# The convolution norm: sums of squares as rows, the inverse root spread through memory

## The chip, the cores and the metric

The kernel runs on one core of one Trainium2 chip. The metric is device time in microseconds (us) of one execution; lower is better. Three runs of the kernel before took 2366.22, 2369.10 and 2373.38 us. The engines are named as the profile names them: PE (matrix products), PEld (its weight loads), DVE, ACT and POOL (elementwise work), SP (the queue that issues most of the transfers).

## The reference

One decoder block over 2048 tokens of 1024 channels, all in float32. The part that matters here is the convolution branch behind the depthwise convolution:

```python
def layer_norm(x, w, b):
    xf = x.astype(jnp.float32)
    mu = jnp.mean(xf, axis=-1, keepdims=True)
    var = jnp.mean(jnp.square(xf - mu), axis=-1, keepdims=True)
    return (xf - mu) * lax.rsqrt(var + EPS) * w.astype(jnp.float32) + b.astype(jnp.float32)
...
        u = a * jax.nn.sigmoid(b)
        u = depthwise_causal_conv(u, conv_w, conv_b)
        u = jax.nn.silu(layer_norm(u, conv_ln_w, conv_ln_b)).astype(dt)
        u = u * jax.nn.silu(g_conv)
        y_conv = u @ w_conv_out
...
        y_attn = o @ w_attn_out
        y = jax.nn.sigmoid(m_conv) * y_conv + jax.nn.sigmoid(m_attn) * y_attn
        out = y @ w_out
```

Per token there is one mean and one variance over 1024 channels, an inverse root of the variance, and then 1024 products with it.

## The kernel before, in words

Activations are kept transposed: channels lie on the 128 partitions, tokens along the row. A product in float32 accuracy is made of three products of halves of the numbers (a high part and a low part), so each matrix product appears three times.

The change lies in the last third of the program. There the tokens are cut into four quarters of 512 (t = 0 to 3), and two loops of 32 blocks each follow one another.

* **The ya loop** (the attention projection): block 8t + dm is 12 products (`project`, L1399) for the quarter t and 128 output channels dm; DVE then makes `yt` from the block's bank and a loaded tile `ma`, and SP stores `yt`.
* **The yc loop** (the convolution projection): block 8t + dm is 24 products on the tiles `u0`...`u7` (high `h`, low `l`) of the quarter t; DVE makes `mc` from the bank and a loaded tile `mc`, adds it to a loaded `yl`, and SP stores `yl`.

Both loops take their banks by dm from three names (z, s, o) with two banks each, so a block can start when the work on an earlier block's bank is done on DVE: in the ya loop block 24 takes the bank of block 19, for example. The tiles `ma` and `mc` have three buffers, `yl` four, `gg` (the silu gate's input of the norm) three. SP issues its transfers strictly in the order written, and waits in place when a buffer is not yet free or a value not yet there.

The convolution norm is made inside these loops, by the class `Norm`, one object for each quarter. Its steps are:

* `load`: the convolution's output `d` comes from memory (two buffers, so quarter t + 2 waits for quarter t);
* `mean` (L1421 to L1429): a product with ones gives the sums (`pm`), DVE takes the mean off, ACT squares, DVE sums the eight squares into `red`, which holds for each token 128 partial sums on 128 partitions;
* `variance` (L1435 to L1437, and L114, L115): four products with `red` as the weights and a column of ones turn `red` into a column of 128 tokens each (`pc`), DVE copies it to `stf`, POOL takes the power -1/2 (`rsqrt_cols`, two instructions);
* `spread` (L1444, L1447): four products with the column stretched over 128 columns and the identity give the inverse root on all 128 partitions (`pr`), ACT copies it to `rs`;
* `apply(k)` for k = 0 to 7 (L1452 to L1461): DVE multiplies `d` by `rs` (`vf`), ACT takes silu (`tv`), DVE multiplies by `gg` (`vf` again), ACT makes the high part `u_kh`, DVE the low part `u_kl`.

Where a step stands among the products is set by `at_block(n, m, f)`: step f is written ahead of product m of block n. On PE the program's order is kept as written. On DVE, ACT, POOL and SP the builder orders the instructions by its own estimate of when each can start, and the order is then fixed. Quarters 0 and 1 have their steps in the ya loop, quarters 2 and 3 in the yc loop; quarter 0 must be ready for yc block 0, quarter 1 for block 8, quarter 2 for block 16, quarter 3 for block 24. Beside the norm, DVE, ACT and SP prepare the weights of the final product in yc blocks 10 to 30 (`wo_raw`, `wot`, `woB`).

## Time and profile before

| what | value |
|---|---|
| runs shown | 2366.22, 2369.10, 2373.38 us, median 2369.1 |
| profiled execution | 2370.1 us, of it span 2368.3 us |
| granted clock of PE, mean | 0.997 |
| PE, DVE, ACT, POOL busy in the span | 98%, 73%, 43%, 35% |
| ya loop | about 1928 to 2027 us of the span |
| yc loop | about 2027 to 2212 us |

The span is the time from the first to the last instruction; the rest of the execution lies outside it. In the tables a line such as L1399 is a line of the kernel before, "idle" is time in which an engine did nothing ahead of an instruction, and the releaser is what ended that wait. "xN" counts records; one float32 product of full width makes two of them.

### The profile page before, as it was taken

The page shows a single profiled execution, that of the slowest core. Times are in us where ns is not written, and L with a number is a line of the kernel's source. Part 1 is how long each engine was busy: PE and PEld are TensorE (multiplying, and loading weights), DVE is VectorE, ACT ScalarE, POOL GpSimd, SP SyncE. Part 2 cuts the span into 40 slices and gives each one's busy share as a digit, 9 for nine tenths or more (in the row PEclk, how much of TensorE's full clock was granted, in tenths as well). Part 3 has the DMA queues.
Part 4 walks back from the last instruction along what each step waited for, and adds up shares of the span by engine and source line. Part 5 has one row for each costly group of instructions (what it writes and reads, how often), then busy time and mean ns, then how long its engine had stood idle before and what let it go on. Part 6 is the DMA issues. An engine that isn't in the chain of part 4 may idle for free.

```text
span 2368.3 us, 38785 instructions
## 1 busy us (share of the span) xinstructions
PE 2325.8 (98%) x12421; PEld 2083.0 (88%) x12421; DVE 1737.0 (73%) x4104; ACT 1020.9 (43%) x2825; POOL 836.1 (35%) x976
## 2 busy tenths in 40 slices
PE   6999999999999999999999999999999999999999
PEld 4899999999999999997888888788888888878887
DVE  7855655555556777776699999989968768787654
ACT  5733343343344555456444444544444444332221
POOL 4321111111111111123677778656556730000221
PEclk9999999999999999999999999999999999999999
DMA  7733544454552222144535445745444569876552
GB/s 279 241 116 117 160 125 144 149 169 149 158 162 67 60 80 67 47 123 154 170 135 176 160 152 195 241 130 151 139 150 134 165 213 330 292 236 204 185 167 102
DMA packets 354121, 378.57 MB, mean 160 GB/s; under 512 B 27688, under 2 KB 249176, under 8 KB 353918
## 3 DMA queue, kind: packets, MB, share of 16 engines
q1 hardware_dynamic: 312622, 314.05, 42.6%
q10 hardware_dynamic: 41296, 62.05, 7.5%
q8 instruction: 99, 1.62, 0.3%
q14 instruction: 104, 0.85, 0.1%
HBM read 235.34 MB, written 140.64 MB: 159 GB/s over the span
## 4 chain that ended last, share of the span: by engine, by line
PE 88%; DMA 4%; DVE 4%; ACT 2%; issue 1%; POOL 1%; SPq 0%; ACTq 0%; DVEq 0%; POOLq 0%
PE pz L549 31%; PE paab L1091 7%; PE yc L1399 6%; PE oa L1681 4%; PE pcab L1091 4%; PE pag_mc_d L1091 4%; PE pag_g_d L1091 3%; PE pag_ma_d L1091 3%; PE po L684 3%; PE ps L635 3%; PE ya L1399 2%; PE pcg_g_d L1091 2%; PE oc L1681 2%; PE pbab L1091 2%; PE paag L1091 2%; PE pcg_mc_d L1091 2%
## 5 line engine op out<-in xcount | busy, mean ns | idle before, releaser
L549 PE MATMUL pz<-wh_u,hT_lo 128*128 128x384 f32 x1504 | 525.2, 349 | 2.5 <-DVE hT_lo L371 2.4
L549 PE MATMUL pz<-wh_u,hT_hi 128*128 128x384 f32 x1504 | 505.6, 336 | 1.3 <-ACT hT_hi L369 1.3
L549 PE MATMUL pz<-wl_u,hT_hi 128*128 128x384 f32 x1504 | 505.8, 336 | 0.0
L114 POOL TENSOR_SCALAR st<-st 128x2 f32<-128x2 f32 x192 | 44.9, 234 | 797.0 <-ACT sq L572 796.7
L586 DVE SCALAR_TENSOR_TENSOR qk<-pz,st,wqk 128x128 f32<-128x128 f32 x384 | 116.9, 346 | 265.0 <-POOL st L115 260.8
L549 PEld LDWEIGHTS pz<-wh_u,hT_lo 128*128 128x128 f32 x1504 | 283.2, 188 | 4.0 <-DVE hT_lo L371 3.7
L549 PEld LDWEIGHTS pz<-wh_u,hT_hi 128*128 128x128 f32 x1504 | 283.8, 189 | 2.2 <-ACT hT_hi L369 1.9
L549 PEld LDWEIGHTS pz<-wl_u,hT_hi 128*128 128x128 f32 x1504 | 282.8, 188 | 0.5 <-issue 0.5
L627 ACT ACTIVATE qkT<-ptq 128x256 f32<-128x256 f32 x192 | 73.8, 384 | 358.1 <-PE ptq L620 302.5
L1169 DVE SCALAR_TENSOR_TENSOR ce<-us,pair_taps,ce 128x512 f32<-128x512 f32 x240 | 180.9, 754 | 6.5
L1140 DVE SCALAR_TENSOR_TENSOR ce<-ut,chan,ce 128x512 f32<-128x512 f32 x240 | 179.8, 749 | 0.0
L1055 POOL TENSOR_TENSOR slT<-wT,shT 128x512 fp32r<-128x512 f32 x107 | 143.8, 1345 | 79.8 <-ACT shT L1054 79.5
L1153 DVE SCALAR_TENSOR_TENSOR cq<-ut,chan,cq 128x512 f32<-128x512 f32 x208 | 156.0, 750 | 1.0
L1054 ACT ACTIVATE shB<-wB 128x512 fp32r<-128x512 f32 x130 | 82.1, 631 | 161.7 <-PE paab L1091 51.7
L115 POOL TENSOR_TENSOR st<-st,mhalf 128x2 f32<-128x2 f32 x192 | 140.1, 729 | 15.9
L572 ACT ACTIVATE sq<-pz 128x128 bf16<-128x128 f32 x384 | 106.1, 276 | 78.7 <-PE pz L549 68.9
L1054 ACT ACTIVATE shT<-wT 128x512 fp32r<-128x512 f32 x110 | 69.4, 631 | 160.9 <-POOL wT L1046 32.0
L1055 POOL TENSOR_TENSOR slB<-wB,shB 128x512 fp32r<-128x512 f32 x85 | 111.9, 1317 | 76.1 <-ACT shB L1054 73.8
L684 PE MATMUL po<-lv,pT 128*128 128x128 f32 x596 | 96.8, 274 | 0.0
L684 PEld LDWEIGHTS po<-lv,pT 128*128 128x128 f32 x596 | 90.9, 190 | 0.6 <-issue 0.5
L593 DVE TENSOR_TENSOR t<-qk,tab 128x256 f32<-128x256 f32 x192 | 82.5, 430 | 5.7
L1055 POOL TENSOR_TENSOR slT<-wB,shT 128x512 fp32r<-128x512 f32 x57 | 75.1, 1324 | 28.4 <-ACT shT L1054 28.3
(783 smaller groups left out, 6163.2 us busy)
## 6 DMA issues: line engine op xcount, KB each, us to landing
wB<-in_w_in_dram SPq DMA_DIRECT2D x154, 256.0 KB, 3.2
qkv_d<-qkv SPq DMA_DIRECT2D x128, 192.0 KB, 2.3
wT<-tT_d SPq DMA_DIRECT2D x88, 256.0 KB, 2.7
tT_d<-wB ACTq DMA_DIRECT2D x66, 256.0 KB, 2.7
lqk<-qkv_d SPq DMA_DIRECT2D x128, 128.0 KB, 2.3
raw_u<-in_w_in_dram SPq DMA_DIRECT2D x84, 192.0 KB, 3.6
acc_d<-osb SPq DMA_DIRECT2D x128, 65.0 KB, 2.0
part<-acc_d ACTq DMA_DIRECT2D x64, 130.0 KB, 2.4
```

Source lines behind the costliest of these rows:

```text
L115: nc.gpsimd.tensor_tensor(dst, scratch[:, :n], mhalf[:, :n], op=ALU.pow)
L549: nc.tensor.matmul(pz[:, :width], part(a, k, P * j, P), w[:, :width], start=(m == 0), stop=(m == 23))
L586: nc.vector.scalar_tensor_tensor(qk[:, 2 * i : 2 * i + 2].rearrange("p a b -> p (a b)"), pz[:, P * i : P * i + P], st[:, 2 + i : 3 + i], w ...
L684: nc.tensor.matmul(po[:, :P], box["pT"][:, P * i : P * i + P], vt, start=(i == 0), stop=(i == nk - 1))
L1054: nc.scalar.activation(h, q[name], AF.Copy)
L1055: eng.tensor_tensor(l, q[name], h.bitcast(F32), op=ALU.subtract)
L1091: nc.tensor.matmul(ps, w, x, start=(m == 0 and ps.name not in first), stop=(m == 11 and not more), skip_group_check=True)
L1140: stt(box["e"], e[:, 1 + j : 513 + j], chan[:, cb, 2 * j : 2 * j + 1], box["e"], op0=ALU.mult, op1=ALU.add)
L1153: stt(box["o"], o[:, 2 + j : 514 + j], w, psum_o, op0=ALU.mult, op1=ALU.add)
L1169: stt(dst, box["both"][:, 1 + j : 513 + j], pair_taps[:, cb, j : j + 1], box["e"], op0=ALU.mult, op1=ALU.subtract if j == 0 else ALU.add)
L1399: nc.tensor.matmul(pz, w, xx, start=(m == 0), stop=(m == len(terms) - 1))
L1681: nc.tensor.matmul(ps, y, w, start=(m == 0 and ps.name not in begun), stop=(m == 11 and not more), skip_group_check=True)
```

## The change

The sums of squares are made the other way round. Ones (32 columns of them) are now the weights, and a piece of `red` with 128 tokens is what streams: each of the four products gives a row of 128 sums, repeated on 32 partitions, and the four lie on partitions 0, 32, 64 and 96 of one bank. DVE copies the bank to `row`. Then memory does the rest: four writes of one row each make a line of 512 values in `var_d`, one read brings it back as 128 x 4 (`stf`), POOL takes the inverse root of that, one write puts it into a second line of 512, and one read copies that line to all 128 partitions (`rs`). The four identity products and ACT's copy are gone. All seven transfers are issued by SP.

POOL's two instructions now belong to `spread`. The steps stand at other places in the yc loop: `spread` of quarter 2 six products later in block 7, `variance` of quarter 3 in block 15 ahead of product 6 (it was block 14, product 12), `spread` of quarter 3 in block 16. The eight `apply` of quarter 2 go from 9.0 to block 14 in steps of 19 products (they stood in blocks 8 to 15, one in each), those of quarter 3 from block 17 to 22 in steps of 18.

```diff
+    var_d = [[dram.tile([512], F32, name=f"var{i}{t}_d") for i in range(2)] for t in range(S // 512)]
...
             pc = bank("t", f"pc{t}")
             for i in range(4):
-                nc.tensor.matmul(pc[:, i : i + 1], self.red[:, P * i : P * i + P], ones[:, :1], start=True, stop=True)
-            st = self.st = ap.tile([P, 12], F32, tag="stf", name=f"stf{t}")
-            nc.vector.tensor_copy(st[:, :4], pc[:, :4])
+                nc.tensor.matmul(pc[32 * i : 32 * i + 32, :P], ones[:, :32], self.red[:, P * i : P * i + P], start=True, stop=True)
+            row = ap.tile([P, P], F32, tag="row", name=f"row{t}", bufs=1)
+            nc.vector.tensor_copy(row, pc[:, :P])
+            for i in range(4):
+                nc.sync.dma_start(var_d[t][0][None, P * i : P * i + P], row[32 * i : 32 * i + 1, :])
+            self.st = ap.tile([P, 12], F32, tag="stf", name=f"stf{t}")
+            nc.sync.dma_start(self.st[:, :4], var_d[t][0].rearrange("(p i) -> p i", i=4))
+
+        def spread(self):
+            t, st = self.t, self.st
             rsqrt_cols(st[:, 4:8], st[:, :4], 4, st[:, 8:12])
-
-        def spread(self):
-            t = self.t
-            pr = bank("t", f"pr{t}")
-            for i in range(4):
-                nc.tensor.matmul(pr[:, P * i : P * i + P], self.st[:, 4 + i : 5 + i].to_broadcast([P, P]), ident,
-                                 start=True, stop=True)
+            nc.sync.dma_start(var_d[t][1].rearrange("(p i) -> p i", i=4), st[:, 4:8])
             self.rs = ap.tile([P, 512], F32, tag="rs", name=f"rs{t}")
-            nc.scalar.activation(self.rs, pr, AF.Copy)
+            nc.sync.dma_start(self.rs, var_d[t][1][None, :].to_broadcast([P, 512]))
...
-                    (8, 3, "load"), (9, 3, "mean"), (14, 3, "variance"), (15, 3, "spread")):
+                       (8, 12, 3, "load"), (9, 12, 3, "mean"), (15, 6, 3, "variance"), (16, 12, 3, "spread")):
...
-            at_block(KC * (t - 1) + k, 17, lambda t=t, k=k: norms[t].apply(k))
+            at = 24 * KC * (t - 1) + (17 + 24 * k if t == 1 else 24 + 19 * k if t == 2 else 36 + 18 * k)
+            at_block(at // 24, at % 24, lambda t=t, k=k: norms[t].apply(k))
```

Outside the norm's surroundings all engines keep their order. POOL's order is the same throughout. Three places show what moved. In the names the first digit is the quarter, the second the block or the k; a number behind the last underscore only tells buffers apart.

On PE, around quarter 3's variance, before (yc blocks 14 and 15):

```order
L1399 MATMUL yc1_6_24492<-u1_3l_23987,wc1h0_23759 128x512
L1399 MATMUL yc1_6_24492<-u1_3h_23986,wc1l0_23761 128x512
L1435 MATMUL pc3_24505<-ones_92,red3_24255 128x1 x4
L1399 MATMUL yc1_6_24492<-u1_4h_24029,wc1h1_23760 128x512
L1399 MATMUL yc1_6_24492<-u1_4l_24030,wc1h1_23760 128x512
...
L1399 MATMUL yc1_7_24544<-u1_3h_23986,wc1l0_23761 128x512
L1444 MATMUL pr3_24557<-ident_87,stf3_24510 128x128 x4
L1399 MATMUL yc1_7_24544<-u1_4h_24029,wc1h1_23760 128x512
```

and the same place on PE after:

```order
L1400 MATMUL yc1_7_24560<-u1_1h_23896,wc1h0_23771 128x512
L1400 MATMUL yc1_7_24560<-u1_1l_23897,wc1h0_23771 128x512
L1400 MATMUL yc1_7_24560<-u1_1h_23896,wc1l0_23773 128x512
L1436 MATMUL pc3_24567<-red3_24269,ones_100 32x128 x4
L1400 MATMUL yc1_7_24560<-u1_2h_23947,wc1h0_23771 128x512
L1400 MATMUL yc1_7_24560<-u1_2l_23948,wc1h0_23771 128x512
```

The four `pc3` stand 18 products later, in block 15, and the four `pr3` are gone.

On SP, ahead of yc blocks 9 to 12, before (stores `y_d<-yl`, loads of `mc`, `yl` and of quarter 2's `gg`):

```order
L1654 DMA yl1_1_24238<-ya_d_81 128x512
L1661 DMA y_d_82<-yl0_6_24088 128x512
L1652 DMA mc1_1_24236<-mc_d_77 128x512
L1654 DMA yl1_2_24314<-ya_d_81 128x512
L1452 DMA gg2_3_24377<-g_d_76 128x512
L1452 DMA gg2_4_24424<-g_d_76 128x512
L1661 DMA y_d_82<-yl0_7_24140 128x512
L1652 DMA mc1_2_24312<-mc_d_77 128x512
L1654 DMA yl1_3_24357<-ya_d_81 128x512
```

and after (`d3` is quarter 3's load, `var02_d` and `var12_d` are quarter 2's two lines in memory):

```order
L1440 DMA var02_d_91<-row2_24120 1x128 x4
L1416 DMA d3_24219<-u_d_75 128x2x512
L1664 DMA y_d_82<-yl0_6_24100 128x512
L1416 DMA d3_24219<-u_d_75 128x2x512
L1442 DMA stf2_24126<-var02_d_91 128x4
L1655 DMA mc1_1_24239<-mc_d_77 128x512
...
L1664 DMA y_d_82<-yl0_7_24156 128x512
L1655 DMA mc1_2_24326<-mc_d_77 128x512
L1447 DMA var12_d_92<-stf2_24126 128x4
L1657 DMA yl1_3_24371<-ya_d_81 128x512
L1664 DMA y_d_82<-yl1_0_24204 128x512
L1449 DMA rs2_24191<-var12_d_92 128x512
```

The seven small transfers now stand among the stores and loads of blocks 6 to 11, and the loads of quarter 2's `gg` from k = 3 on stand behind them.

On DVE, where quarter 2's last parts and quarter 3's last sum of squares are made, before:

```order
L1461 TENSOR_TENSOR u2_6l_24527<-vf2_6_24521,u2_6h_24526 128x512
L1429 TENSOR_TENSOR red3_24255<-red3_24255,sq3_6_24279 128x512
L1660 TENSOR_TENSOR yl1_4_24400<-yl1_4_24400,mc1_4_24398 128x512
L1461 TENSOR_TENSOR u2_7l_24577<-vf2_7_24571,u2_7h_24576 128x512
L1429 TENSOR_TENSOR red3_24255<-red3_24255,sq3_7_24283 128x512
```

and after:

```order
L1463 TENSOR_TENSOR u2_2l_24353<-vf2_2_24347,u2_2h_24352 128x512
L1430 TENSOR_TENSOR red3_24269<-red3_24269,sq3_7_24297 128x512
L1463 TENSOR_TENSOR u2_3l_24391<-vf2_3_24385,u2_3h_24390 128x512
...
L1438 COPY row3_24572<-pc3_24567 128x128
L1456 SCALAR_TENSOR_TENSOR vf2_7_24533<-d2_23757,chan_113,rs2_24191 128x512
L1460 SCALAR_TENSOR_TENSOR vf2_6_24495<-tv2_6_24497,gg2_6_24493 128x512
L1460 SCALAR_TENSOR_TENSOR vf2_7_24533<-tv2_7_24535,gg2_7_24531 128x512
L1463 TENSOR_TENSOR u2_6l_24501<-vf2_6_24495,u2_6h_24500 128x512
L1662 SCALAR_TENSOR_TENSOR mc1_7_24556<-mc1_7_24556,yc1_7_24560 128x512
L1463 TENSOR_TENSOR u2_7l_24539<-vf2_7_24533,u2_7h_24538 128x512
```

Quarter 3's last sum now comes when quarter 2 has its parts up to k = 2, and quarter 2's last part stands behind `mc` of block 15, one block ahead of its use; from quarter 2's first `vf` (the instruction behind quarter 3's mean on DVE) to that last sum there are 29 instructions, to the last part 48.

4 lines of the change are left out of this document (2 added, 2 removed).

## The prediction, on record before the run

> **What bounds the kernel now.** I read the page's engine shares and its chain first, then the list of what PE waited for, then the stages around the change, then the chain itself there.
>
> ```profile
> PE 2325.8 (98%) x12421; PEld 2083.0 (88%) x12421; DVE 1737.0 (73%) x4104; ACT 1020.9 (43%) x2825; POOL 836.1 (35%) x976
> ...
> PE 88%; DMA 4%; DVE 4%; ACT 2%; issue 1%; POOL 1%; SPq 0%; ACTq 0%; DVEq 0%; POOLq 0%
> ```
>
> PE is busy for 98% of the span and is 88% of the chain that ended last. So a PE instruction taken away is worth its time, and anything else is worth only what PE waits for it.
>
> ```profile
> PE paab L1091 <- ACT spare_hi L1217: 4.1, 1, 4.1
> ...
> PE pc L1435 <- DVE red L1429: 2.8, 1, 2.8
> ...
> PE ptq L620 <- DVE lqk L596: 2.2, 1, 2.2
> ...
> PE pr L1444 <- POOL stf L115: 0.4, 1, 0.4
> ```
>
> Columns: total wait, times, longest. Two of PE's waits stand in the steps that change: 2.8 us for a `red`, 0.4 us for POOL.
>
> ```profile
> 1966.00:2027.00 61.00, 60.64 (x281) 49.95 (x280) 47.82 (x79) 24.82 (x40) 3.38 (x4) 1.00 0.93 312
> 2027.00:2083.00 56.00, 56.00 (x252) 45.90 (x251) 46.10 (x75) 23.61 (x38) 1.26 (x2) 1.00 0.84 278
> 2083.00:2125.00 42.00, 39.16 (x174) 32.26 (x173) 36.12 (x55) 11.46 (x19) 1.63 (x2) 0.96 0.72 243
> ```
>
> By stage (busy PE, PEld, DVE, ACT, POOL, then clock and the transfer engines' share): here DVE is 78 to 86% busy and the transfer engines 72 to 93%. The change puts four transfers in a row, and DVE behind them, into the stretch with the least room.
>
> ```profile
> 1966.37 0.79 PE pc L1435 x8
> ...
> 1972.75 0.89 PE pr L1444 x8
> ...
> 2019.42 1.16 PE pr L1444 x8
> ...
> 2063.67 0.79 PE pc L1435 x8
> 2064.46 5.61 PE yc L1399 x24
> 2070.07 0.89 PE pr L1444 x8
> ...
> 2112.79 1.07 PE pc L1435 x8
> 2113.86 7.14 PE yc L1399 x24
> 2121.00 0.89 PE pr L1444 x8
> 2121.90 89.80 PE yc L1399 x396
> ```
>
> The chain by time: start, length, records. All `pc` and `pr` shown lie on it; the `pc` of quarter 1 does not and is counted like the undisturbed ones. One product takes 89.80 / 396 = 0.227 us. Behind the 2.8 us wait 24 products take 7.14 us, against 5.61 behind the undisturbed `pc`:
>
> ```profile
> 2109.80:2112.80 3.00, 0.16 (x2) 0.04 (x1) 2.84 (x5) 0.56 (x1) 0.00 (x0) 1.00 0.89 261
> ...
> 2114.00:2116.00 2.00, 2.00 (x5) 1.53 (x5) 1.00 (x1) 0.00 (x0) 0.00 (x0) 0.50 0.99 346
> ```
>
> The granted clock falls to 0.50 after that wait. A wait of this size thus costs itself and 7.14 - 5.61 = 1.5 us more. The list above also has waits of 2.2 us and less; I take the extra 1.5 from 2.8 us on. In the Trainium skill, "TensorE: Matmul & The Clock Gate", Part 1 on the HAM clock gate, half rate comes after about one idle window of 3.4 us; this trace has it after 2.8 us. By the page a wait of 3 us costs 3 us, and the sum below would come out 1.5 us lower.
>
> **What PE gains.** The spreading products go: 0.89 + 1.16 + 0.89 + 0.89 = 3.8 us, with POOL's 0.4 us wait in front of one. ACT's copies of `pr` go too; ACT is under half busy and they were on no path but this.
>
> The four `pc` cost 0.79 + 0.79 + 0.79 + 1.07 = 3.4 us. In their place stand four products of 32 columns of weights and 128 columns streamed, onto four different groups of partitions. One at a time they would cost what `pr` costs, 0.89 us for eight records. The same form exists at the program's start, with 256 columns:
>
> ```profile
> 35.89 1.50 PE L314 MATMUL ada<-first_lo,first_hi 128*32 128x256 f32 x24
> ```
>
> 24 records in 1.50 us is 0.50 for eight, so the pieces run side by side; half the columns would be 0.25. The weight loads do not halve, so I take 0.40, between the two and nearest to that row: 3.4 - 1.6 = 1.8 us gained, and between a loss of 0.1 and a gain of 2.4 at the ends.
>
> The 2.8 us wait for `red` and its 1.5 us of slow clock go if quarter 3's last sum is ready in time (below). Together 3.8 + 0.4 + 1.8 + 2.8 + 1.5 = 10.3 us.
>
> **What memory costs.** PE no longer waits for the statistics directly. DVE does, at each quarter's first `vf`, with every later DVE instruction behind it; and SP does, at three of the seven transfers, with later loads behind. The price of one hop (issue to landing) of so small a transfer inside this stretch is in no row. From the window of the two loops, and one from the page:
>
> ```profile
> ma<-ma_d SPq DMA_DIRECT2D x29, 256.0 KB, 5.8
> ...
> gg<-g_d SPq DMA_DIRECT2D x32, 256.0 KB, 4.3
> ...
> yl<-ya_d SPq DMA_DIRECT2D x32, 256.0 KB, 3.2
> ...
> d<-u_d SPq DMA_DIRECT2D x16, 512.0 KB, 7.6
> ...
> wo_raw<-in_w_out_dram SPq DMA_DIRECT2D x4, 1024.0 KB, 7.5
> ```
>
> ```profile
> acc_d<-osb SPq DMA_DIRECT2D x128, 65.0 KB, 2.0
> ```
>
> Ends: 2.0 us (small, where the queue is quiet) and 7.6 us (behind 2 MB of its own kind). I take 5.8 in the ya loop and 4.3 in the yc loop, the rows of the transfers among which the hops stand.
>
> ```profile
> 1970.22 0.69 DVE L1513 SCALAR_TENSOR_TENSOR yt<-ma,ya 128x512 f32<-128x512 f32 x1
> ...
> 1971.31 0.42 SPq L1507 DMA_DIRECT2D ma<-ma_d  x1
> ```
>
> ```profile
> L114 POOL TENSOR_SCALAR stf<-stf x4: 226/418/602, 1969.2 to 2118.7; 128x4 f32<-128x4 f32 x4
> L115 POOL TENSOR_TENSOR stf<-stf,mhalf x4: 1026/1032/1522, 1969.5 to 2119.4; 128x4 f32<-128x4 f32 x4
> ```
>
> ```profile
> 2041.00:2063.00 22.00, 22.00 (x99) 18.22 (x98) 22.00 (x37) 11.03 (x18) 0.00 (x0) 1.00 0.70 228
> ```
>
> An SP issue is 0.4 us, POOL's two instructions 1.5 us, and a DVE that never idles does 37 instructions in 22.0 us, 0.60 each.
>
> *Quarter 0.* The fourth row write stands behind the store of the `yt` that DVE ends at 1970.9, so it issues at about 1972. Four hops and POOL: 1972 + 4 x 5.8 + 1.5 = 1996.7, when DVE can go on with the first `vf`. The `yt` of block 19 is the 12th instruction from there, done at 2003.9. PE wants its bank for block 24, which starts 150 products after `pc` with one `pm` (0.86, an estimate from its place in the chain) between: 1966.4 + 0.4 + 34.1 + 0.9 = 2001.8. So PE waits about 2 us; since the row writes bring almost no bytes of their own and each hop may be some tenths shorter than `ma`'s, I take 1 us. At 4.3 us a hop nothing waits.
>
> *Quarter 1.* Its rows leave at about 2018 and are back at about 2040, when DVE is just through quarter 2's mean; 44 instructions (26.4 us) bring its last part to 2066. Block 8 wants it at about 2074. Hidden, with 8 us to spare.
>
> *Quarter 2, where it is tight.* Block 16 starts before at 2121.9 + 12 x 0.227 = 2124.6, after at 2124.6 - 10.3 = 2114.3. Its 23rd product wants the last part, `u2_7l`, at 2114.3 + 5.0 = 2119.3, and `pc3`, 18 products and itself ahead of block 16, wants the last `red3` at 2109.8. DVE's `row2` stands 40 instructions behind quarter 1's first `vf`: 2040 + 24 to 26 = 2065.5. Issues 1.6, four hops 17.2, POOL 1.5 and about 2 us for the three 512 KB `d3` loads that stand among the first two hops: `rs2` at 2088.
>
> ```profile
> 2096.33 2.36 DVE L1550 TENSOR_TENSOR wo_raw<-wo_raw,gate 128x1024 f32<-128x1024 f32 x2 [2.56 <-DMA wo_raw<-in_w_out_dram]
> ```
>
> ```profile
> SPq L1654 <- DMA y_d<-yl: 68.2, 27, 4.4
> ...
> SPq L1452 <- DVE vf L1458: 6.4, 2, 6.1
> ```
>
> From 2088 to the last `red3` are 29 instructions: 17.4, plus 1.2 because the pair on `wo_raw` takes 2.36, plus 1.6 since `wo_raw`'s load now stands behind `rs2` on SP (issued 2084.5, landed 2092, reached by DVE at 2090.4). That is 2108.2, in time for `pc3`: the old wait goes. To `u2_7l` are 48 instructions, 2088 + 28.8 + 1.2 + 1.6 = 2119.6, already 0.3 late. SP makes it later. Its load of `gg` for k = 3 waits for the first second-`vf` of the quarter (2095), as such loads did before for up to 6.1 us, and the load for k = 7 stands four rounds of store, wait for the landing and reload behind: the wait is 68.2 / 27 = 2.5 us by the first row, four issues 1.6. So 2097.5 + 4 x 4.1 + 0.8 = 2114.7, landed 2119.0; the product with it, ACT's high part and DVE's low part are three instructions of 0.6 to 0.7, done at 2121.1. With the longest wait of that row (4.4) in place of the mean it is 2128.7. I take 3 us late, nearer the mean, and the 1.5 us of slow clock.
>
> *Quarter 3.* `pc3` at 2110, `row3` at 2115, four hops, POOL and a 1 MB `wo_raw` load between: 2140. 37 instructions more: 2162. Block 24 wants it at 2114.3 + 43.5 + 5.0 = 2163, later still by what was lost before. Hidden, barely.
>
> **Sum.** -10.3 + 1 + 3 + 1.5 = -4.8 us on the profiled execution's 2370.1 us (span 2368.3 and 1.8 around it), which is 1.0 above the median of the runs shown. On the median: 2369.1 - 4.8 = 2364.3, rounded 2364.
>
> **Rivals.**
>
> *No wait at all.* With hops like `yl`'s 3.2 us, quarter 0 is back at 1986, and `rs2` at about 2084, when quarter 3's mean has hardly left DVE; `u2_7l` is ready at 2116. Then the full 10.3 us stay: 2359. For it: rows of 128 numbers weigh nothing. Against: they queue among loads that take 4.3 and 5.8. The Trainium skill, "DMA: Bandwidth & Descriptors", Anatomy of one DMA, gives a fixed cost of about 2.0 us whatever the size; by that four hops cost 8 us and this rival holds. The trace agrees with it only where the queue is quiet (2.0); no row shows a small transfer in this stretch.
>
> *Slower: the hops pile up.* At 7.6 us a hop, quarter 0 is back at 1972 + 30.4 + 1.5 = 2003.9 and block 24 of the ya loop waits 2003.9 + 7.2 - 2001.8 = 9.3 + 1.5 us; `rs2` comes at 2065.5 + 1.6 + 30.4 + 1.5 = 2099, `u2_7l` 30.0 behind it, and block 16 waits 9.7 + 1.5. Together 22 against 10.3: 2381. It decides from hops of about 6 us in both loops on, where the two waits reach 10. For it: a transfer share of 0.93 in the ya loop, and DVE at 86% cannot catch up. Against: 7.6 is the price of half a megabyte.
>
> *The rows don't run side by side.* Then each `pc` costs 0.89 and 2.0 us of the gain is missing: 2366. Row L314 speaks against it.
>
> **Numbers.** Forecast (one or two short waits, a net gain of 1 to 9 us): 0.45. No wait: 0.25. Hops pile up: 0.25. Not side by side: 0.05. The measurement tells about 0.3%, 7 us, from no change. Faster than that are the first rival and a little of the forecast, 0.29; slower by that the second without its mildest part, 0.24; the rest, 0.47, is the same. Range: from the full gain with `pc` at its best, 2358, to the pile-up's 2381; about 0.1 is left out at each end.
>
> **What would show it.** `pr` gone, eight records of `pc` at 0.3 to 0.5 us, no wait of `pc` for `red`. A new PE wait in block 16 on `u_6l` or `u_7l`, released by DVE or ACT, with a clock below 1 behind it, and a smaller one on a bank near block 24 of the ya loop. On DVE new idle ahead of the first `vf`, released by the `rs` transfer. I am wrong if the `var_d` transfers land in 2 to 3 us, or if SP, held at its three waits, starves DVE of `ma`, `mc` or `gg` elsewhere.

## The result: 2375.2 us, 0.16% slower

Twenty runs of the changed kernel have a median of 2375.18 us (2370.37 to 2380.41), twenty of the kernel before on the same chip 2371.52 us (2366.22 to 2376.40). The ratio is 1.0016, with a 95% interval of 1.0009 to 1.0022. That is inside the 0.3% that the prediction called "the same", but it is a loss of 3.7 us where a gain of 4.8 was forecast. The profiled execution took 2374.1 us, 4.0 more than that of the kernel before (span 2372.3 against 2368.3).

The page of the changed kernel, engine shares and chain:

```profile
PE 2325.5 (98%) x12389; PEld 2079.8 (88%) x12389; DVE 1737.2 (73%) x4104; ACT 1017.7 (43%) x2821; POOL 835.3 (35%) x976
...
PE 84%; DMA 5%; DVE 4%; issue 2%; ACT 1%; POOL 1%; SPq 0%; ACTq 0%; DVEq 0%; POOLq 0%
```

PE's busy time is unchanged over the whole span although the 16 `pr` products (32 records) are gone. In the two loops it fell by 2.3 us only, from 280.1 to 277.8, since a slower clock, below, filled part of the gap; the other 2.0 us came in the stages outside. PE's share of the chain fell from 88% to 84%. The list of what PE waited for, the rows that belong to the two loops:

```profile
PE pc L1436 <- DVE red L1430: 5.5, 1, 5.5
...
PE yc L1400 <- DVE u_6l L1463: 1.9, 1, 1.9
PE yc L1400 <- DVE wc1l L1261: 1.3, 1, 1.3
...
PE yc L1400 <- DVE u_7l L1463: 0.2, 1, 0.2
PE ya L1400 <- DVE yt L1515: 0.2, 1, 0.2
```

The wait for `red` that was to vanish has doubled, from 2.8 to 5.5 us. PE's own rows there, and the clock behind the two waits (columns as in the prediction's table by stage):

```profile
2063.37 0.43 PE L1436 MATMUL pc<-red,ones 128*32 128x128 f32 x8
...
2118.10 0.65 PE L1436 MATMUL pc<-red,ones 128*32 128x128 f32 x8 [5.53 <-DVE red L1430]
...
2131.19 0.50 PE L1400 MATMUL yc<-u_6l,wc0hi 128*128 128x512 f32 x1 [1.87 <-DVE u_6l L1463]
```

```profile
2118.10:2120.00 1.90, 1.90 (x11) 1.32 (x12) 1.90 (x4) 0.69 (x1) 0.00 (x0) 0.50 0.74 179
2120.00:2122.00 2.00, 2.00 (x6) 1.52 (x6) 2.00 (x4) 0.98 (x3) 0.00 (x0) 0.50 0.86 302
2122.00:2124.00 2.00, 2.00 (x9) 1.60 (x8) 1.84 (x4) 1.01 (x2) 0.00 (x0) 0.77 0.35 130
...
2131.20:2134.00 2.80, 2.56 (x8) 1.81 (x9) 1.74 (x3) 0.06 (x1) 0.00 (x0) 0.85 0.75 138
2134.00:2137.00 3.00, 3.00 (x9) 2.33 (x8) 0.00 (x0) 0.00 (x0) 0.00 (x0) 0.57 0.98 370
```

Eight `pc` records take 0.43 us, so the four pieces do run side by side. The clock stands at 0.50 for 3.9 us behind the first wait and at 0.57 behind the second: (1 - clock) x time gives 2.4 and 1.7 us lost.

Why DVE was late is in its own timeline, here from quarter 2's `row` to quarter 3's last sum:

```profile
2072.05 0.29 DVE L1438 COPY row<-pc 128x128 f32<-128x128 f32 x1
...
2086.50 1.29 DVE L1426 SCALAR_TENSOR_TENSOR d<-pm,d 128x512 f32<-128x512 f32 x2 [1.43 <-DMA d<-u_d]
2097.65 1.42 DVE L1456 SCALAR_TENSOR_TENSOR vf<-d,chan,rs 128x512 f32<-128x512 f32 x2 [9.86 <-DMA rs<-var_d]
2098.98 0.68 DVE L1430 TENSOR_TENSOR red<-red,sq 128x512 f32<-128x512 f32 x1
...
2117.27 0.69 DVE L1430 TENSOR_TENSOR red<-red,sq 128x512 f32<-128x512 f32 x1
```

DVE stands still for 9.9 us ahead of quarter 2's first multiplication, with seven of quarter 3's sums behind it. The trips themselves, on SP:

```profile
2074.98 2.92 SPq L1440 DMA_DIRECT2D var_d<-row  x4
...
2082.49 0.33 SPq L1442 DMA_DIRECT2D stf<-var_d  x1
...
2088.10 0.32 SPq L1447 DMA_DIRECT2D var_d<-stf  x1
...
2092.70 0.38 SPq L1449 DMA_DIRECT2D rs<-var_d  x1
```

From the last of the four writes (2077.9) to the read is 4.6 us, from the read to POOL (2086.7) 4.2, from the write to the last read 4.6, and from that to DVE 4.9. The third of these holds SP's own order too: up to 2091.4 SP stood 2.9 us at a load of `yl` that waited for a store, and issued the last read as soon as its turn came.

The account between the first product of the ya loop and the first product of the last loop: 283.4 us before, 286.9 after, 3.5 more. Gone are 3.8 us of `pr`, 1.8 of `pc` and the 0.4 for POOL, together 6.0. New are 2.7 at `pc3`, 0.9 of slow clock behind it (2.4 against 1.5), 2.1 at `u_6l` and `u_7l` with 1.7 of slow clock, and 1.3 at `wc1l`, together 8.7. The 0.2 at `yt` stands in block 11 of the ya loop, ahead of the first changed instruction, and the kernel before waits 0.1 there too. The balance of +2.7 leaves 0.8 unnamed.

### The profile page after: what moved, and what is told of

Read it like the earlier page. It is cut to its first block, busy times and chain, and to the rows that moved or that the text cites. A ratio compares the mean times of both kernels' runs of the same rounds, so it can differ in the third digit from the quotient of the medians.

```text
span 2372.3 us, 38760 instructions
## 1 busy us (share of the span) xinstructions
PE 2325.5 (98%) x12389; PEld 2079.8 (88%) x12389; DVE 1737.2 (73%) x4104; ACT 1017.7 (43%) x2821; POOL 835.3 (35%) x976
## 4 chain that ended last, share of the span: by engine, by line
PE 84%; DMA 5%; DVE 4%; issue 2%; ACT 1%; POOL 1%; SPq 0%; ACTq 0%; DVEq 0%; POOLq 0%
PE pz L550 30%; PE paab L1092 7%; PE pcab L1092 4%; PE pag_mc_d L1092 4%; PE oa L1684 4%; PE yc L1400 4%; PE pag_g_d L1092 3%; PE pag_ma_d L1092 3%; PE po L685 3%; PE ps L636 3%; PE ya L1400 2%; PE pcg_g_d L1092 2%; PE oc L1684 2%; PE pbab L1092 2%; PE pcg_mc_d L1092 2%; PE paag L1092 2%
## 5 line engine op out<-in xcount | busy, mean ns | idle before, releaser
L550 PEld LDWEIGHTS pz<-wh_u,hT_hi 128*128 128x128 f32 x1504 | 283.4, 188 | 3.2 <-ACT hT_hi L370 1.8
```

The costliest lines, as they stand in the source:

```text
L550: nc.tensor.matmul(pz[:, :width], part(a, k, P * j, P), w[:, :width], start=(m == 0), stop=(m == 23))
```

## The experiments

Kernels of one group ran on one chip and are compared with the kernel before on that chip. The ratio is to the kernel before, with its 95% interval; the last column is PE's wait at `pc3` in the profile.

| kernel | median us | ratio | at `pc3`, us |
|---|---|---|---|
| the changed kernel | 2375.2 | 1.0016 (1.0009 to 1.0022) | 5.5 |
| new places alone | 2376.5 | 1.0014 (1.0005 to 1.0022) | 0; 5.7 at `pr3` |
| memory alone, old places | 2376.2 | 1.0019 (1.0010 to 1.0027) | 11.5 |
| two trips by columns | 2400.6 | 1.0116 (1.0103 to 1.0129) | 10.7 |
| quarter 1's root in quarter 2 | 2379.8 | 1.0032 (1.0021 to 1.0043) | 7.0 |
| the changed kernel again | 2375.7 | 1.0011 (1.0001 to 1.0020) | 5.3 |
| trips issued by ACT | 2380.8 | 1.0034 (1.0021 to 1.0046) | 0 |
| trips issued by POOL | 2379.5 | 1.0032 (1.0020 to 1.0044) | 5.5 |
| two trips by rows | 2376.9 | 1.0021 (1.0013 to 1.0030) | 3.0 |
| sums first, four trips | 2374.0 | 1.0006 (0.9996 to 1.0017) | 0 |
| whole row, old places, 4 bytes added | 2383.8 | 1.0045 (1.0032 to 1.0057) | 5.3 |
| whole row, new places, 4 bytes added | 2377.5 | 1.0018 (1.0009 to 1.0027) | 0.6 |
| whole row, old places | 2376.7 | 1.0017 (1.0008 to 1.0026) | 5.6 |
| whole row, new places | 2369.1 | 0.9986 (0.9978 to 0.9995) | 1.6 |
| kernel before, `wo_raw` later | 2368.6 | 0.9982 (0.9973 to 0.9991) | 0 |
| whole row, new places, `wo_raw` later | 2365.6 | 0.9973 (0.9964 to 0.9981) | 0 |
| kernel before and 4 bytes | 2380.7 | 1.0036 (1.0023 to 1.0050) | 0.9 |
| kernel before and 32 bytes | 2382.9 | 1.0032 (1.0012 to 1.0052) | 2.3 |
| kernel before and 64 bytes | 2376.7 | 1.0028 (1.0015 to 1.0040) | 0 |

### The two halves apart

New places alone: the kernel before with the changed kernel's table.

```diff
...
-                    (8, 3, "load"), (9, 3, "mean"), (14, 3, "variance"), (15, 3, "spread")):
...
+                       (8, 12, 3, "load"), (9, 12, 3, "mean"), (15, 6, 3, "variance"), (16, 12, 3, "spread")):
...
```

> Everything of the kernel before (columns of pc, identity products pr, no memory) at the changed kernel's places: quarter 3's variance 6 products after the start of block 15 of the yc loop, spread and multiplications a block later. Theory of the chain (the loss comes from rs of quarter 2 landing at 2097 us and DVE standing 9.9 us before vf2_0): rs of quarter 2 is there some 20 us before it is wanted, DVE does not stand, PE's wait of 2.8 us for the last sum of quarter 3 and its 1.5 us of slow clock vanish, nothing else moves: 4 us below the kernel before, about 2367. Rival (the new places themselves crowd DVE's stream at the end, so that sums and multiplications come late whatever brings the inverse root): PE's wait at pc3 stays near 5 us and the waits at u2_6l and u2_7l show again, no faster than before, 2371 to 2375.

Memory alone: the changed kernel with that line, and the multiplications, at the places of before.

> The changed kernel's pieces side by side and its way by memory, at the places of the kernel before (quarter 3's variance at product 12 of block 14, multiplications of quarter 2 from product 17 of the first block on). Theory of the chain: rs of quarter 2 lands at about the same 2097 us, DVE stands at vf2_0 as long or longer, and pc3 is wanted 18 products, some 4 us, earlier: PE's wait at pc3 grows from 5.5 to about 9.6 us, and u2_6l and u2_7l wait at least as now: about 4 us above the changed kernel, 2379. Rival of the places: with the old places the wait is smaller than 5.5 us, and the time is below the changed kernel, about 2366 by my own sum without the two block waits.

Each half alone costs about as much as both together. In the kernel with the new places alone the wait at `pc3` is gone, as expected, and stands one step later:

```profile
PE pr L1444 <- POOL stf L115: 6.9, 2, 5.7
```

DVE's copy of `pc3` had fallen behind two pairs of scalings of `wo_raw`, each behind a load (4.0 and 0.9 us of idle time), so POOL and then `pr3` came late. The prediction of 2367 was wrong, and so was the rival that the wait at `pc3` would stay.

With memory alone, the wait at `pc3` grows to 11.5 us, the expected direction (9.6 expected), because it is asked for 18 products earlier while DVE stands even longer:

```profile
DVE vf L1456 <- DMA rs<-var_d: 12.4, 1, 12.4
```

The time rises far less than the wait, to a ratio of 1.0019. The waits at `u_6l` and `u_7l` in block 16 are gone, as one would expect where PE is held longer ahead of them.

One thing came out of the built programs here. The part of the change that moves the multiplications moves almost nothing. They hold no product, and DVE, ACT and SP are ordered by the builder's estimate: written at the places of before, the changed kernel has the same order on every engine but for two loads of SP that change places (`yl2_2` and `gg3_1`). Of the new places only those that hold products count, `variance` and, in the kernel before, `spread`.

### The trips: how many, and on which queue

Quarter 1's root in quarter 2, which was to take away DVE's wait and leave the trips:

```diff
-            nc.vector.scalar_tensor_tensor(v, self.d[:, k], chan[:, k, TAPS + 1 : TAPS + 2], self.rs,
+            nc.vector.scalar_tensor_tensor(v, self.d[:, k], chan[:, k, TAPS + 1 : TAPS + 2], norms[1].rs if t == 2 else self.rs,
```

> The changed kernel, in which quarter 2's eight multiplications take quarter 1's inverse root (so quarter 2 of the convolution's norm is scaled by the wrong quarter's values); all transfers of quarter 2 stay, and DVE does not wait for their end. Theory of the chain: DVE goes through vf2_0 without its 9.9 us, the sums of quarter 3 end before 2110 us, and PE's waits at pc3, u2_6l and u2_7l with their slow clock go, 5.5 + 2.0 + 2.1 + 1.6 = 11.2 us at most, about 2364. Rival (DVE is late there for other reasons: the loads gg and wo_raw, its own work, or SP being held): the waits move by less than 3 us, 2372 or more.

Neither theory's number came: `pc3` waited 7.0 us, and another 5.0 us appeared in the last loop, at an `xt`. Without the dependence the builder put five of quarter 2's multiplications ahead of quarter 3's mean, and DVE then waited 7.4 us there for `gg`:

```profile
2090.86 0.69 DVE L1460 SCALAR_TENSOR_TENSOR vf<-tv,gg 128x512 f32<-128x512 f32 x1 [6.23 <-DMA gg<-g_d]
2092.73 0.69 DVE L1460 SCALAR_TENSOR_TENSOR vf<-tv,gg 128x512 f32<-128x512 f32 x1 [1.17 <-DMA gg<-g_d]
```

An edit that removes a wait also reorders DVE here, so this run doesn't isolate the wait. The next two ask whether SP, held at the trips, is the cause. They issue all seven transfers from another queue, here ACT's for the first of them; in the other kernel it is `nc.gpsimd`, POOL's.

```diff
-                nc.sync.dma_start(var_d[t][0][None, P * i : P * i + P], row[32 * i : 32 * i + 1, :])
+                nc.scalar.dma_start(var_d[t][0][None, P * i : P * i + P], row[32 * i : 32 * i + 1, :])
```

> The changed kernel with the seven small transfers issued by ACT in place of SP; nothing else is written differently. SP's loads no longer stand behind a waiting trip, and the trips don't stand behind SP's loads and stores: quarter 2's row writes go right behind row2, and rs2 lands at about 2072.3 + 1.6 + 4 x 4.6 + 1.5 = 2094 instead of 2097.6. Theory that SP's order is half of the loss: DVE's wait at vf2_0 falls by 4 us or more, pc3's wait from 5.5 to about 2, 2369. Theory that the trips themselves are the loss: no more than 1 us changes, 2374. Rival (ACT now stands at the trips and holds squares, silu and high parts back): DVE and PE wait for ACT, 2378 or more.

> The changed kernel with the seven small transfers issued by POOL, which has only 1.3 us of work in this stretch, so that neither SP's loads nor ACT's work stand behind a waiting trip. Theory that SP's order is what hurts: rs2 lands at 2094 or earlier, DVE's wait at vf2_0 falls to 6 us or less, no gg comes late, pc3 waits under 2 us, nothing waits in block 16: 2366. Theory that the four trips themselves are the loss: DVE's wait and pc3's stay within 2 us of 9.9 and 5.5, 2374. Rival (transfers issued by POOL are slower than SP's): DVE's wait grows, 2380.

ACT is the wrong place: its rival of 2378 or more came true. It stood 8.6 us at the row writes; PE waited 5.8 us for quarter 1's `u_7h`, came to `pc3` late enough not to wait there, and waited another 4.9 us for `u_6l` in block 16. POOL, which has little else to do there, shows the price of a trip with no other transfer ahead of it (idle time of POOL until the trip before had landed, in quarter 2):

```profile
2075.72 0.58 POOL L1442 DMA_DIRECT2D stf<-var_d  x1 [4.68 <-DMA var_d<-row]
2081.64 0.22 POOL L115 TENSOR_SCALAR stf<-stf 128x4 f32<-128x4 f32 x1 [5.35 <-DMA stf<-var_d]
...
2089.14 0.55 POOL L1449 DMA_DIRECT2D rs<-var_d  x1 [4.99 <-DMA var_d<-stf]
```

Here a trip costs about 5 us although nothing else stands in its queue. Over all four quarters POOL's 28 transfers took 2.2 to 6.4 us from issue to landing, with a median of 5.2. In this kernel the idle time ahead of quarter 2's `vf` is gone, and a hole of the same size opens at a pair of `wo_raw` that the builder now puts ahead of it, again with quarter 3's sums behind:

```profile
2098.67 2.36 DVE L1553 TENSOR_TENSOR wo_raw<-wo_raw,gate 128x1024 f32<-128x1024 f32 x2 [11.14 <-DMA wo_raw<-in_w_out_dram]
```

`pc3` again waits 5.5 us. So neither SP's row nor `rs2` alone is what holds the sums: whatever DVE's order puts ahead of them holds them. New in this kernel is a wait in the last loop, where PE stands 2.8 us for an `xt`.

Fewer trips, first with `pc` as columns and the inverse root straight behind, then one write of the columns and one read:

```diff
...
-            nc.sync.dma_start(var_d[t][1].rearrange("(p i) -> p i", i=4), st[:, 4:8])
+            nc.sync.dma_start(var_d[t][1].rearrange("(i p) -> p i", p=P), st[:, 4:8])
```

> The changed kernel with the columns of pc and the inverse root on POOL straight behind, as before; only the way from the four columns to all partitions goes by memory, one write and one read in place of four trips. Theory of the chain: two trips of 4.6 us and their places in SP's row fall away, rs of quarter 2 lands some 10 us earlier, at about 2087, DVE does not stand, and the waits at pc3 (5.5 us), u2_6l and u2_7l (2.1 us) and their slow clock (3.6 us) vanish; pc costs 1.8 us more per the four stages than side by side: about 2366, 9 us below the changed kernel. A write of single 4-byte elements could take longer than a trip of 512 bytes: at 5 us longer DVE would still stand 5 us, and the time would be about 2371. Rival (it is not the arrival of rs but the transfers' load on SP and the queues, or the places): little change, 2373 to 2376.

That write goes in single elements of 4 bytes, and the price named as a risk was far too low. SP issued quarter 2's read 13.9 us behind the write (2089.0 and 2102.9); DVE waited 14.1 us, and PE waited another 7.8 us for `yt` in the ya loop and 8.1 us for `xt` in the last loop. It says nothing on the chain. The second form keeps the rows and reads them back onto all partitions; ACT takes the root, DVE the reciprocal:

```diff
-            nc.sync.dma_start(self.st[:, :4], var_d[t][0].rearrange("(p i) -> p i", i=4))
+            nc.sync.dma_start(self.rs, var_d[t][0][None, :].to_broadcast([P, 512]))
...
+            nc.scalar.activation(self.rs, self.rs, AF.Sqrt, bias=eps_col)
+            nc.vector.reciprocal(self.rs, self.rs)
```

> The changed kernel with two trips in place of four: rows are written as now and read back onto all 128 partitions at once, as the variance; ACT takes the root and DVE the reciprocal (3.35 us) there; its constant lies in the old unused tile. Theory of the chain (length of the trips): rs2 lands two trips, 9 us, and 1.5 us of POOL earlier, 1.3 + 0.7 of ACT and 3.4 of DVE come on top: DVE can go on 5 us earlier than now, pc3 waits about 1 us, u_6l and u_7l nothing: 2367. Rival (any trip holds SP and DVE at these places): pc3 and block 16 wait as long as now, 2375.

At the same places `pc3` waits 1.6 us with no trip (below), 3.0 with two and 5.5 with four. But the time does not follow. In its profile other waits of PE are new or longer: 2.4 us at `yt` in the ya loop, 1.2 at quarter 0's `u_6l` and `u_7l`, and 1.8 at an `xt` in the last loop. That the reciprocals on DVE, 3.35 us each, are behind them is likely but not shown.

The changed kernel once more, to see how far such waits vary:

> The changed kernel once more, beside the next three on the same chip, to see how far the length of its waits differs from one profile to the next. If the waits come from the order of the work, pc3's wait lies within 2 us of 5.5 and DVE's at vf2_0 within 2 us of 9.9; if they come from chance in the transfers, they differ by more. 2375.

Both stay well within 2 us: 5.3 us at `pc3`, 10.7 us of DVE at quarter 2's `vf`. Smaller waits do vary: block 16 waits 3.3 us here for `u_6l`, against 1.9 and 0.2 for `u_6l` and `u_7l`. So a difference of 1.4 us in one wait between two profiles says little.

### DVE's order

The decisive experiment keeps all four trips on SP and turns DVE's order round. It also moves quarter 2's multiplications behind quarter 3's mean. The builder then puts quarter 3's squares earlier on ACT, and some loads of `gg`, `wo_raw` and `yl` at other places on SP, so DVE's order is not all that differs.

```diff
+            if t == 2 and k == 0:
+                nc.vector.scalar_tensor_tensor(self.rs[:, :1], norms[3].red[:, :1], 0.0, self.rs[:, :1],
+                                               op0=ALU.mult, op1=ALU.add)
...
-            at = 24 * KC * (t - 1) + (17 + 24 * k if t == 1 else 24 + 19 * k if t == 2 else 36 + 18 * k)
+            at = 24 * KC * (t - 1) + (17 + 24 * k if t == 1 else 42 + 16 * k if t == 2 else 36 + 18 * k)
...
+        if k == 0:
+            nc.vector.scalar_tensor_tensor(w[:, 0, :, 0], norms[2].ul[4][:, :2].bitcast(F32), 0.0, w[:, 0, :, 0], op0=ALU.mult, op1=ALU.add)
```

> The changed kernel with all its trips; only DVE's order is turned round: two tiny DVE instructions (times zero, so no value changes) make quarter 2's first multiplication depend on quarter 3's last sum, and the first scaling of wo_raw on quarter 2's fifth low part. Theory of the order (DVE stands 9.9 us for rs2 with sums behind it that have all they need): the eight sums are done while rs2 travels, pc3 finds red3 ready, its 5.5 us and 2.0 us of slow clock go; u2_7l is 39 instructions behind rs2's landing at 2097.6, ready at 2122 to 2126, 0 to 4 us later than wanted, as now: 2367, and 2363 if block 16 does not wait. Rival (the trips hold SP and so every load, and DVE will wait elsewhere for what comes late): pc3's wait goes but waits of 8 us or more appear at u_6l or u_7l: 2375 or more.

All of PE's waits in the two loops:

```profile
PE yc L1400 <- ACT u_6h L1465: 4.1, 1, 4.1
PE yc L1400 <- DVE u_4l L1466: 1.3, 1, 1.3
PE yc L1400 <- DVE u_6l L1466: 1.1, 1, 1.1
PE yc L1400 <- DVE wc1l L1261: 0.6, 1, 0.6
...
PE yc L1400 <- DVE u_5l L1466: 0.5, 1, 0.5
PE yc L1400 <- ACT wc1h L1260: 0.4, 1, 0.4
```

And two of DVE's, where it comes to `rs2` and to a `gg` of quarter 2:

```profile
2101.95 0.16 DVE L1456 SCALAR_TENSOR_TENSOR rs<-red,rs 128x1 f32<-128x1 f32 x1 [0.98 <-DMA rs<-var_d]
...
2115.80 0.69 DVE L1463 SCALAR_TENSOR_TENSOR vf<-tv,gg 128x512 f32<-128x512 f32 x1 [5.19 <-DMA gg<-g_d]
```

The 5.5 us at `pc3` are gone although `rs2` landed 4.3 us later than in the changed kernel (2101.9 against 2097.6), so the order in which DVE, and with it ACT, meets the sums and `rs2` was their cause. But 7.0 us appear in block 16, and the clock averages 0.70 from there to 2140 us:

```profile
2123.05:2140.00 16.95, 11.24 (x32) 7.92 (x33) 14.23 (x20) 2.67 (x5) 0.00 (x0) 0.70 0.82 274
```

Theory and rival were each half right. `rs2` comes too late for somebody: for quarter 3's sums if DVE meets it first, for quarter 2's parts if the sums go first, and there a `gg` that came 5.2 us late added to it. The median lies 1.5 us above the kernel before, but its interval overlaps that of the changed kernel, so a gain in time isn't shown, only that the wait moves.

The same handle without any trip: in the kernel before, the three scalings of `wo_raw` are made to follow quarter 3's column (`norms[3].st`), and in the whole-row kernel quarter 3's `rs`.

```diff
+        if k < 3:
+            nc.vector.scalar_tensor_tensor(w[:, 0, :, 0], norms[3].st[:, :2], 0.0, w[:, 0, :, 0], op0=ALU.mult, op1=ALU.add)
```

> The kernel before; DVE's scalings of wo_raw (three pairs) get a dependence on quarter 3's column of variances and so stand behind it, where they stood ahead of quarter 3's sums and of that copy. Theory of the order: the pair of 2.36 us and its wait of 2.6 us no longer stand ahead of the last sum, pc3's wait of 2.8 us and 1.5 us of slow clock go: 4 us below the kernel before, 2367. Rival (something else sets the last sum, such as gg or the squares): pc3 waits 2 us or more, 2370 to 2372; or wo_raw's late scaling holds the last loop: above 2372.

The wait at `pc3` is gone; the forecast of 2367 was met at 2368.6, a ratio of 0.9982 (0.9973 to 0.9991). So the 2.8 + 1.5 us at `pc3` that the forecast counted on were to be had in the kernel before by an edit of DVE's order, without the change. The builder moved some loads of `wo_raw`, `gg` and `yl` on SP with it; what they add is not separated.

### No memory and no identity products

```diff
-            for i in range(4):
-                nc.tensor.matmul(pc[:, i : i + 1], self.red[:, P * i : P * i + P], ones[:, :1], start=True, stop=True)
...
+            nc.tensor.matmul(pc, ones, self.red, start=True, stop=True)
+            self.rs = ap.tile([P, 512], F32, tag="rs", name=f"rs{t}")
+            nc.scalar.activation(self.rs, pc, AF.Sqrt, bias=eps_col)
+            nc.vector.reciprocal(self.rs, self.rs)
...
```

> No trips through memory and no identity products, at the places of the kernel before: one product per quarter with ones as the weights and the whole of red streaming puts each token's sum on all 128 partitions, ACT takes the root of it and DVE the reciprocal, straight into rs. Four such products cost what pm costs, some 0.86 us each, 3.4 together like the four pc before. Theory (DVE's stream sets when red of quarter 3 is ready): of the 3.8 us of pr and 0.4 us for POOL only what lies behind pc3 is gained, the rest goes into a longer wait at pc3, some 6 us in place of 2.8: 2369 to 2371. Rival (PE's own work is what counts): 4 us below the kernel before, 2367. Rival (root on ACT and reciprocal on DVE are dear, or ACT changes its tables): above 2374.

> The whole-row product, ACT's root and DVE's reciprocal, at the changed kernel's places. Nothing of PE waits for POOL or for a trip. Theory of the chain (memory's trips made the waits; the places alone moved the wait to pr3): pc3 finds red ready, there is no pr3 to wait, quarter 2's parts are ready 10 us ahead of block 16: 3.8 + 0.4 + 2.8 + 1.5 = 8.5 us below the kernel before, 2363. Rival (the places crowd DVE so that red3, u2_6l, u2_7l or the weights of the last product come late): 2370 or more.

Both came far above what was expected, the second with hardly a wait left in the two loops. Products that the edit doesn't touch had become dearer, in the last loop 395 to 397 ns in place of 389. The suspect is the new constant of the root (`eps_col`), 4 bytes on each partition ahead of most other tiles. Such a tile alone, in the kernel before:

```diff
+    shift = consts.tile([P, 1], F32, name="shift")
+    nc.gpsimd.memset(shift, 0.0)
```

> The kernel before with one unused tile of 4 bytes on each partition among its constants, so that every tile made later lies 4 bytes further on; no instruction but its one memset is added. Theory of the addresses: products of the last loops take 395 to 397 ns against 389, and the time rises by 8 to 14 us: 2380 to 2386. Rival (it was ACT's root and its tables or DVE's reciprocal that cost the time in the first whole-row kernels): no change, 2371.

A group of products of the last loop in the kernel before, and the same group with 4 bytes more among the constants:

```profile
L1681 PE MATMUL oa<-wohiT,yh 128*128 128x512 f32 x64 | 24.9, 389 | 0.0
```

```profile
L1683 PE MATMUL oa<-wohiT,yh 128*128 128x512 f32 x64 | 25.3, 396 | 0.0
```

With nothing else changed, the kernel before becomes 8 us slower (ratio 1.0036), although its wait at `pc3` is shorter. The order on every engine is that of the kernel before. In the built program a tile of 4 bytes takes up 32, so the tiles behind it lie 32 bytes further on, not 4, and about a third of all tiles don't move. The products that became slower are those of the ya, yc and last loops; others with 512 columns keep a median of 389 ns. In the ya loop of this one trace the products that read `ai0lo`, which did not move, take 389 ns, and those that read `ai_1h`, which did, 396:

```profile
L1401 PE MATMUL ya<-ai0lo,wah 128*128 128x512 f32 x32 | 12.5, 389 | 0.0
...
L1401 PE MATMUL ya<-ai_1h,wah 128*128 128x512 f32 x24 | 9.5, 396 | 0.0
```

Whether the start of a tile must be a multiple of something was asked with 32 and 64 bytes.

> The kernel before with an unused tile of 32 bytes in place of 4. If tiles need to start at a multiple of 32 bytes, products take 389 ns and the time is 2371; if 64 bytes are needed, 396 ns and 2380.

> The same with 64 bytes. If a multiple of 64 bytes is enough, 389 ns and 2371; if any shift costs, whatever its size, 396 ns and 2380.

Neither rule holds. A tile of 32 bytes places every other tile as the one of 4 bytes does, so that kernel is in effect a repetition: 396 ns again, and 0.32% in place of 0.36%. Moved by 64 bytes, the same group's products take 394 ns and the time is 0.28% longer. Both shifts cost. In the kernel before, all operands of these products start at a multiple of 128 bytes, which neither shift keeps; whether that is what matters no run asked, so it stays open what the addresses must meet.

With the constant in an old, unused tile, so that all tiles keep their addresses, and the changed places or those of before:

```diff
-    edge.tile([P, 120], F32, name="edge")
+    eps_t = edge.tile([P, 120], F32, name="edge")
+    nc.gpsimd.memset(eps_t, EPS)
+    eps_col = eps_t[:, 0:1]
```

> The whole-row kernel at the changed kernel's places once more, with the small constant of the root kept in an old, unused tile instead of a new one of 4 bytes, so that every other tile keeps its address on the partitions. Theory (the new 4 bytes moved all tiles behind them and made products dearer: the last loop's products took 395 to 397 ns against 389, and the start of the ya loop, the two loops and the last loop came 5.6, 4.8 and 3.9 us late against what their instructions add up to): the 14 us come back, 2363, below the kernel before. Rival (the products are dearer because of the load of DVE, 3.35 us for each reciprocal, or of ACT): 2377 as before the repair.

> The same repair with the places of the kernel before. Against the run before this one it tells what the changed places alone bring when no trip and no identity product stands between them. Theory (DVE sets when red of quarter 3 is ready, and the old place asks for it 4 us earlier): pc3 waits some 5 us again with slow clock behind, 6 us above the same kernel at the changed places: 2369. Rival (the places do not matter): 2363 to 2365.

The products take 389 ns again. At the changed places the kernel runs at 0.9986 (0.9978 to 0.9995), faster than the kernel before and, by the ratios, than the changed kernel; its median of 2369.1 brings back 8 of the expected 14 us. At the places of before it is 1.0017. PE's wait at `pc3` tells the two apart, 1.6 us at the new places and 5.6 at the old; with the clock at 0.50 and 0.75 behind the longer wait alone, that is about 5.8 of the 7.5 us between their medians:

```profile
PE pc L1436 <- DVE red L1431: 1.6, 1, 1.6
```

```profile
PE pc L1436 <- DVE red L1431: 5.6, 1, 5.6
```

So the new place of quarter 3's variance is a good one once no `pr3` and no trip hangs on it. DVE does four reciprocals of 3.35 us more here, 13.4 us in all, and PE waits no longer in the two loops than in the kernel before (3.1 us against 3.2). So the amount of DVE's work is not what bounds this stretch. Last, the kernel at the new places with `wo_raw` behind quarter 3's reciprocal (the edit of the kernel before, with `norms[3].rs[:, :2]`):

> The whole-row kernel at the changed places, constant in the old tile, with the three scalings of wo_raw behind quarter 3's reciprocal on DVE. Theory of the order: the wait of 1.6 us at pc3 goes and nothing takes its place: 1.5 to 2 us below the same kernel without this, 2367. Rival (wo_raw's late scaling makes the weights of the last product late): waits at oa, 2370 or more.

PE's only wait left in the two loops:

```profile
PE ya L1401 <- DVE yt L1508: 1.7, 1, 1.7
```

2365.6 us, a ratio of 0.9973 (0.9964 to 0.9981), is the fastest version: 7 us below the kernel before on its chip.

## Why the prediction was wrong

**The step that failed** is the one on quarter 2: "From 2088 to the last `red3` are 29 instructions [...] That is 2108.2, in time for `pc3`: the old wait goes." `rs2` landed at 2097.6, and the last `red3` ended at 2118.0. In place of a gain of 2.8 + 1.5 there was a loss of 2.7 + 0.9, a swing of 7.9 us out of the 8.5 between forecast and result.

The term that was mis-sized in it is the landing of `rs2`, 9.6 us too early, and mostly its start; the 29 instructions from there took the 20.3 us that the prediction counts (20.2). The prediction had `row2` at 2065.5 and 22.5 us from there; the trace has 2072.05 and 25.6. The start is 6.6 us late because quarter 1's first multiplication stood at 2047.8 and not at 2040:

```profile
2041.21 0.42 SPq L1449 DMA_DIRECT2D rs<-var_d  x1
```

```profile
2044.66 0.69 DVE L1261 TENSOR_TENSOR wc1l<-fraw,wc1h 128x512 fp32r<-128x512 f32 x1 [3.35 <-ACT wc1h L1260]
...
2047.77 1.41 DVE L1456 SCALAR_TENSOR_TENSOR vf<-d,chan,rs 128x512 f32<-128x512 f32 x2
```

Quarter 1's last trip was issued only at 2041.2, behind loads of weights and of `yl` on SP. DVE did not stand for it: ahead of the multiplication it stood 3.4 and 0.6 us at `wc1l`, for ACT, and the raw weights came from loads that SP issued at 2038.4 and 2040.4, where the kernel before had issued three such loads by 2036.3. From the multiplication to `row2` DVE then lost only 0.3 us. The sum had let each quarter start its chain on time; in the trace the order of SP and DVE around quarter 1's trips carried over to the start of quarter 2's. Of the other 3.1 us, about 1 is the trips' price, and the rest lies in SP's order, most of it at the row writes, which were all issued only 5.6 us behind `row2`.

**What held.** `pr` gone with POOL's wait, and `pc` at 0.43 us (0.40 predicted): 6.0 us gained, as in the sum. Quarter 2's trips at 4.2 to 4.9 us (4.3). By the fixed cost that the Trainium skill gives in "DMA: Bandwidth & Descriptors", Anatomy of one DMA, such a trip would cost an estimated 2.0 us. The page describes transfers issued by GpSimd; on POOL's queue here the median was 5.2 us, over twice the page's figure, and the shortest 2.2. Block 16 waited 2.1 us with 1.7 of slow clock (3 and 1.5). Quarters 1 and 3 were hidden. Block 24 of the ya loop did not wait, where 1 us was counted, and 1.3 us at `wc1l` were not foreseen; that the two nearly cancel is luck.

**The rivals.** "The hops pile up" gave the right sign by the wrong mechanism: it was to decide from trips of 6 us on, and it was decided at 4.6 by where each chain starts and by what DVE's order puts behind it. "No wait at all" asked for `rs2` at 2084. The prediction did name DVE's later instructions behind the first `vf`; it did not ask what a few microseconds of error in `rs2` would do to sums that stood 29 instructions behind with less than 2 us of slack.

**What stays open.** 0.8 us of the account; which of the late steps on SP delays quarter 1's last trip most; and the rule behind the addresses.

## What to carry to other kernels

Where an engine works in a fixed order, ask first what the order puts behind a value that comes late; the same value a step earlier or later in that order was worth about as much here (2.8 to 5.5 us at `pc3`, and the slow clock behind it) as the instructions saved (5.6). A chain of dependent small transfers in a busy stretch costs its trips and also the start of the next chain, so follow it through every stage and not from one nominal start. When an edit adds a tile, compare the duration of untouched instructions before reading anything else: one unused tile of 4 bytes cost more than the whole change.

## What the runs showed of the hardware

* Tiles that lie 32 or 64 bytes further on, with no instruction but one memset more, raised the products of 512 columns that read them from 389 to between 394 and 397 ns and the time by 0.28 to 0.36%. Products of the same loop whose tiles had not moved stayed at 389.
* The clock fell to 0.50 behind a wait of 2.8 us in the kernel before and to 0.57 behind waits of 1.9 and 0.2 us in the changed one. It stayed at 1.00 behind single waits of 1.3, 1.6 and 1.7 us, and behind one of 2.8 us in the kernel with the trips on POOL's queue, so the length of a wait alone did not decide. In the Trainium skill, "TensorE: Matmul & The Clock Gate", Part 1 on the HAM clock gate, the window is some 3.4 us; here two waits under it lowered the clock.
* A dependent trip of 2 KB or less took 4.2 to 5.4 us in quarter 2, on SP's and on POOL's queue, in a stretch with a transfer share near 0.8; over all quarters POOL's transfers took 2.2 to 6.4 us.
* A reciprocal of 128 x 512 on DVE takes 3.35 us, five times one of its multiplications of that size (0.69).
